# Later drains, squares and norms in the attention half of a two-layer encoder kernel

## The chip, the cores and the metric

One core of one Trainium2 chip runs the whole kernel in one launch. The metric is device time in microseconds (us). TensorE, VectorE, ScalarE, GpSimd and SyncE are called PE, DVE, ACT, POOL and SP, as in the profile; each runs its own instructions strictly in the order of its program, and waits on semaphores for the others. Line numbers are those of the kernel before, unless a line of after is named.

## The reference

Input x is 2048 rows of 1024 channels in float32. Layer A is a gated MLP that ends in x + mixer(x). Layer B, in which the change lies, is chunked attention, 16 heads of 64 channels:

```python
q, z = jnp.split(h @ w_qz, 2, axis=-1)        # h = rms_norm(x, b_norm_g)
sc = einsum('bqhd,bkhd->bhqk', q*scale, k) + rel_bias     # own chunk and the 8 before
o  = einsum('bhqk,bkhd->bqhd', softmax(sc), v)
x  = x + (o * silu(z)) @ w_out
return rms_norm(x, final_norm_g)
```

## The kernel before

The rows are worked on as four tiles t = 0..3 of 512 rows. The last 1100 us are layer B, tile by tile. A tile has eight head pairs p (names such as `pt3_14` are tile 3, head 14); a pair is walked in eight **score steps** u, four query blocks of each of its two heads. One pass of the loop over u (from L1883) does this:

- `score` (L1377), run two steps ahead: PE makes scores `s`, DVE adds the bias and takes the row maximum (L1400), ACT takes the exponential (L1407), DVE the reciprocal (L1410), POOL normalises into `pr` (L1411).
- `flip` (L1416): PE transposes `pr` in five 128x128 matmuls into the PSUM tile `tp` (L1427); ACT copies it to the high part of `pt` (L1431), DVE subtracts for the low part (L1432). There is one `tp` buffer, so the next transposition on PE waits for that DVE instruction.
- `value` (L1437), at u = 4 for the first head and at u = 0 of the next pair for the second: PE forms PV in tile `pv` (L1452). Then comes its **drain**: ACT copies half of it to `ot` (L1461), DVE adds it into `og32` (L1462), and after a pair's second head DVE gates with `Z` (L1469) and SP stores `og` (L1474). For the last two pairs `last_og` gates into `A_hh` instead (L1568).

Between these, PE is filled with slices of a generator: the projections `pj` of the next pair, whose weights are split into a high half on ACT (L229) and a low half on DVE (L230), and the **output products** `bo` of the tile before. These are a Strassen scheme in phases 1, 7, 2, 6, 5, 4, 3, each for two row pairs jp: three matmuls for each product (L112 to L114, high x high, low x high, high x low), right operands `wh_bo` and `wl_bo` (`whbo` and `wlbo` in the last tile), left operands split into `Sho`/`Slo` or `Qho`/`Qlo` (L338, L343).

`o_evict` (L1666) turns the phase products into output blocks (r, c) of 128x512: phases 2 and 5 give blocks (0,0) and (1,1): DVE adds the product to the residual rows `oc` loaded from `x1d` (L1760), POOL adds `ou` (L1762). Phases 4 and 3 give (1,0) and (0,1): DVE adds the product (L1780), then POOL adds the residual rows `or` that `fetch` loaded (L1782). `done` then appends the block's sum of squares on ACT (`jk`, L1694) to a list, `squares`, that the next score step empties, and its store to `x2d`. Once both blocks of a row group b exist, `finish` goes on the list `finals`: sum (`rr_f`, L1714), root (L126 on DVE, L127 on POOL) and reload `y` from `x2d`; the scaling by `r` and `gf` (L1732) and the store follow later. One entry of `finals` is taken in each score step.

The last tile has no tile behind it to hide its products: 13 slices of them lie in its last pair, the rest follow the last `value`. Its left operands come from `last_open` and `last_sums` (POOL, L1546 and L1557, tiles `A_hl`); `finish` runs at once and the rows `row0` to `row3` go straight to the output.

A list scheduler turns the order in which this code issues into one fixed order for each engine, by its own costs and by the ties of `on_beat` (after the last transposition). SP issues all DMAs of this part, in order, on eight lanes: a DMA waits for the one eight before it, and what stands behind it waits too. The 512-column buffers with tag C (`c_tile`, four of them) hold `oc`, `or` and the squares' output `jk`.

Of the kernel before, what the change touches and what calls it, by code (L numbers as in the profile page):

```python
# [22 lines left out]
NT = S // T  # L23
# [10 lines left out]
def trunk_kernel(  # L34
# [87 lines left out]
    sub, add = ALU.subtract, ALU.add  # L122
# [1150 lines left out]
    with ExitStack() as bctx:  # L1273
# [163 lines left out]
        def value(t, p, hd):  # L1437
# [6 lines left out]
            for i in blocks:  # L1444
                q0, q1 = max(0, i - 4), min(4, i + 1)
                for j in range(2):
                    o = j * 2560 + q0 * 512 + i * P
                    rhs = pt[:, o : o + P]
                    if q1 - q0 > 1:
# [4 lines left out]
                        start=(i == blocks[0] and j == 0), stop=(i == 7 and j == 1),  # L1454
                    )
            if hd == 0:
                og32s[t, p] = sb.tile([P, T], F32, tag="og32", name=f"og32_{t}_{p}", bufs=2)
# [20 lines left out]

        def square_all():
            while squares:  # L1480
                on_beat(squares.pop(0)())

        owed_out = []
# [49 lines left out]
        def last_open():  # L1533
# [17 lines left out]

            return [third] + last_sums(slice(0, 512)) + [lambda: all_of(slice(512, 768))]

# [112 lines left out]
        def o_evict(t):  # L1666
            xa, ya = {}, {}
            last = t + 1 == NT

            def resid(r, c, jp, x_):  # L1670
# [15 lines left out]
            def done(r, c, jp, y):  # L1686
# [11 lines left out]
                if last:  # L1698
                    square()
                else:  # L1700
                    squares.append(square)
                    send(x2d[t][b][:, c * 512 : c * 512 + 512], y)
                if (r, c) in ((1, 0), (0, 1)):
                    if last:
                        finish(b)
                    else:
                        finals.append(lambda: finish(b))

            def finish(b):
                send_all()  # L1710
                square_all()
                r = sm.tile([P, 1], F32, tag="rr", name=f"rr_f{t}_{b}", bufs=4)
# [35 lines left out]
            def evict(ph, jp, ps):  # L1748
# [6 lines left out]
                if ph in (2, 5):  # L1755
# [8 lines left out]
                    if ph == 5:  # L1764
                        tv(x_, ps, x_, op=add)
                        if last:
                            for r, c, y in ((1, 0, y_), (0, 1, x_)):
                                tg(y, y, place(r, c, jp), op=add)
                        elif jp:
                            fetch(1, 0, 0)  # L1770
# [6 lines left out]
                else:  # L1777
                    r, c, y = (1, 0, y_) if ph == 4 else (0, 1, x_)
                    o = place(r, c, jp) if last else y
                    tv(o, ps, y, op=add)  # L1780
                    if not last:
                        tg(y, y, rows.pop(0), op=add)  # L1782
# [84 lines left out]
        for t in range(NT):  # L1867
            for p in range(NPAIR):
# [14 lines left out]
                for u in range(8):  # L1883
# [9 lines left out]
                    elif u == 0 and before:  # L1893
                        value(*before, 1)
                    flip(t, p, u)
                    send_all()
                    square_all()
# [9 lines left out]
                before = t, p  # L1907
        value(*before, 1)
        run(gen)
        run(outs[NT - 1])  # L1910
# [57 lines left out]
```

## Time and profile before

| | |
|---|---|
| median of 3 runs | 2662.0 us (2661.07 to 2662.5) |
| the profiled execution | 2662.61 us, its span 2660.7 us, so 1.9 us lie around the span |
| mean granted PE clock | 0.997 |
| busy PE / DVE / ACT / POOL | 2606.8 / 1888.9 / 1302.4 / 897.6 us (98, 71, 49, 34% of the span) |
| recorded PE waits from 1557 us (the first `pv`) on | 19.8 us |
| matmuls, DVE, ACT, POOL instructions | 12960, 2944, 2303, 874 |

A row of the timeline gives start, duration, engine, line, operation, tiles written and read (buffer numbers left out), and in brackets the idle time before it with what ended that. A row of the waits gives engine, tile and line, what it waited for, then us in total, times, longest. DMA rows on SP are issues; the transfer itself follows.

### The profile page before, as it was taken

The page shows a single profiled execution, that of the slowest core. Times are in us where ns is not written, and L with a number is a line of the kernel's source. Part 1 is how long each engine was busy: PE and PEld are TensorE (multiplying, and loading weights), DVE is VectorE, ACT ScalarE, POOL GpSimd, SP SyncE. Part 2 cuts the span into 40 slices and gives each one's busy share as a digit, 9 for nine tenths or more (in the row PEclk, how much of TensorE's full clock was granted, in tenths as well). Part 3 has the DMA queues.
Part 4 walks back from the last instruction along what each step waited for, and adds up shares of the span by engine and source line. Part 5 has one row for each costly group of instructions (what it writes and reads, how often), then busy time and mean ns, then how long its engine had stood idle before and what let it go on. Part 6 is the DMA issues. An engine that isn't in the chain of part 4 may idle for free. (4 is left out here: it accounts for less than half of the span.)

```text
span 2660.7 us, 37988 instructions
## 1 busy us (share of the span) xinstructions
PE 2606.8 (98%) x12960; PEld 2182.1 (82%) x12960; DVE 1888.9 (71%) x2944; ACT 1302.4 (49%) x2303; POOL 897.6 (34%) x874
## 2 busy tenths in 40 slices
PE   9999999999999999999989999999999999999997
PEld 7788888888888888888878878888888888888886
DVE  5655667766677677757767767778778776877677
ACT  5422243443433434333356456666656655666564
POOL 3511335153252422203234434344333322332235
PEclk9999999999999999999999999999999999999999
DMA  8899999989888878968776587778788667765567
GB/s 299 307 333 332 348 363 325 326 306 358 314 312 296 316 241 323 327 205 270 276 251 218 183 277 237 232 241 269 236 280 276 206 199 225 248 221 159 190 221 260
DMA packets 273856, 718.72 MB, mean 270 GB/s; under 512 B 28800, under 2 KB 68736, under 8 KB 273664
## 3 DMA queue, kind: packets, MB, share of 16 engines
q1 hardware_dynamic: 273664, 716.31, 78.2%
q8 instruction: 103, 1.69, 0.3%
q14 instruction: 89, 0.73, 0.1%
HBM read 531.12 MB, written 174.59 MB: 265 GB/s over the span
## 5 line engine op out<-in xcount | busy, mean ns | idle before, releaser
L112 PE MATMUL P<-T,S 128*128 128x512 f32 x1248 | 495.1, 397 | 1.4 <-ACT S L435 1.4
L114 PE MATMUL P<-T,S 128*128 128x512 f32 x1248 | 489.4, 392 | 0.0
L113 PE MATMUL P<-T,S 128*128 128x512 f32 x1248 | 488.1, 391 | 0.6 <-DVE T L438 0.6
L1411 POOL TENSOR_SCALAR pr<-pr,sl 128x640 f32<-128x640 f32 (+4 forms) x256 | 209.4, 818 | 543.2 <-DVE sl L1410 474.6
L112 PE MATMUL pj<-hh_b,wh_b 128*128 128x512 f32 x768 | 319.2, 416 | 0.0
L114 PE MATMUL pj<-hh_b,wl_b 128*128 128x512 f32 x768 | 304.7, 397 | 0.6 <-DVE wl_b L230 0.5
L113 PE MATMUL pj<-hl_b,wh_b 128*128 128x512 f32 x768 | 302.6, 394 | 0.0
L1407 ACT ACTIVATE pr<-pr,nm 128x640 f32<-128x640 f32 (+4 forms) x256 | 195.4, 763 | 177.9 <-DVE nm L1400 176.0
L114 PEld LDWEIGHTS P<-T,S 128*128 128x128 f32 x1248 | 234.8, 188 | 50.3
L113 PEld LDWEIGHTS P<-T,S 128*128 128x128 f32 x1248 | 235.2, 188 | 46.2 <-DVE T L438 1.0
L112 PEld LDWEIGHTS P<-T,S 128*128 128x128 f32 x1248 | 235.2, 189 | 46.0 <-ACT S L435 1.7
L1432 DVE TENSOR_TENSOR pt<-tp,pt 128x640 fp32r<-128x640 f32 (+4 forms) x256 | 188.4, 736 | 43.0 <-ACT pt L1431 40.2
L1400 DVE CUSTOM_DVE_ANT_0 pr<-s,bias 128x640 f32<-128x640 f32 (+4 forms) x256 | 187.9, 734 | 38.7 <-PE s L1392 34.6
L1431 ACT CAST pt<-tp 128x640 fp32r<-128x640 f32 (+4 forms) x256 | 158.7, 620 | 52.5 <-PE tp L1427 49.5
L1427 PE MATMUL tp<-ident,pr 128*128 128x128 f32 x1120 | 167.1, 275 | 13.0 <-DVE pt L1432 10.0
L114 PEld LDWEIGHTS pj<-hh_b,wl_b 128*128 128x128 f32 x768 | 144.7, 188 | 34.5 <-DVE wl_b L230 2.2
L1427 PEld LDWEIGHTS tp<-ident,pr 128*128 128x128 f32 x1120 | 131.1, 141 | 47.8 <-issue 15.5
L1452 PEld LDWEIGHTS pv<-pt,V 128*128 128x128 f32 x896 | 143.6, 190 | 21.3 <-DVE pt L1432 6.0
L112 PEld LDWEIGHTS pj<-hh_b,wh_b 128*128 128x128 f32 x768 | 145.2, 189 | 17.6 <-ACT wh_b L229 1.2
L113 PEld LDWEIGHTS pj<-hl_b,wh_b 128*128 128x128 f32 x768 | 145.4, 189 | 16.9 <-DVE hl_b L187 0.4
L1452 PE MATMUL pv<-pt,V 128*128 128x256 f32 (+3 forms) x896 | 154.8, 320 | 3.2 <-DVE pt L1432 3.2
L230 DVE TENSOR_TENSOR wl_b<-raw_b,wh_b 128x1024 fp32r<-128x1024 f32 x96 | 120.0, 1251 | 24.3 <-ACT wh_b L229 23.5
(293 smaller groups left out, 5727.7 us busy)
## 6 DMA issues: line engine op xcount, KB each, us to landing
S<-hsd SPq DMA_DIRECT2D x288, 512.0 KB, 5.5
rw<-in_w_a SPq DMA_DIRECT2D x108, 512.0 KB, 6.3
A<-ytd SPq DMA_DIRECT2D x72, 512.0 KB, 5.8
raw_b<-wk SPq DMA_DIRECT2D x72, 512.0 KB, 4.1
hsd<-S SPq DMA_DIRECT2D x56, 512.0 KB, 4.4
V<-vhd SPq DMA_DIRECT2D x56, 512.0 KB, 5.0
bias<-reld SPq DMA_DIRECT2D x64, 320.0 KB, 3.9
va<-vd SPq DMA_DIRECT2D x32, 512.0 KB, 5.6
```

The costliest lines, as they stand in the source:

```text
L112: first = mm(ps, lh, rh, start=first, stop=False)
L113: mm(ps, lh, rl, start=False, stop=False)
L114: mm(ps, ll, rh, start=False, stop=last)
L230: tv(wl[:], raw[:], wh[:].bitcast(F32), op=sub)
L1400: nc.vector.tensor_tensor_reduce(out=pr[:, c0:].rearrange("p (a b) -> p a b", a=nseg), in0=ps[:, :nseg, :w], in1=bias[:, c0:].rearrange("p ...
L1407: nc.scalar.activation(pr[:, c0:], pr[:, c0:], AF.Exp, scale=-1.0, bias=nm[:], accum_out=sl[:])
L1411: nc.gpsimd.tensor_scalar(pr[:, c0:], pr[:, c0:], sl[:], 1.0, op0=ALU.mult, op1=ALU.mult)
L1427: ins = tpose(tp[:, b, :], pr[:, b * P : (b + 1) * P], ident[:])
L1431: nc.scalar.copy(oh, tp[:, b0:5, :].rearrange("p a b -> p (a b)"))
L1432: nc.vector.tensor_tensor(pt[:, 2560 + o + b0 * P : 2560 + o + 640], tp[:, b0:5, :].rearrange("p a b -> p (a b)"), oh.bitcast(F32), op=ALU ...
L1452: mm(po[:, q0 * P : q1 * P], vtl[t, p][:, i, hs], rhs, start=(i == blocks[0] and j == 0), stop=(i == 7 and j == 1),)
```

## The change

It does five things, all in layer B; no instruction is added or taken away (each engine issues as many as before), only their order differs.

1. The drain is cut out of `value` into its own function and put on a list; `drain_all` runs it behind `flip` of the same score step. Behind the last `value` it runs at once.
2. The squares of tiles 0 to 2 go through a second list, `young`, so they are issued two score steps after their sums, not one; `finish` empties both.
3. For tiles 0 and 1 an empty entry stands before `finish` in `finals`: the norm comes one step later.
4. In tile 2 (`at_once`) the residual rows of (1,0) and (0,1) are fetched in phase 5, and POOL adds them there (L1788 of after). Phases 4 and 3 then have only the DVE add.
5. In `last_open` an empty entry stands before `third` (L1546): its two POOL sums come one step later.

```diff
@@ value
+            drains.append(lambda: drain(t, p, hd, po))
+
+        drains = []
+
+        def drain_all():
+            while drains:
+                drains.pop(0)()
+
+        def drain(t, p, hd, po):
+            h = 2 * p + hd
             if hd == 0:
                 og32s[t, p] = sb.tile([P, T], F32, tag="og32", name=f"og32_{t}_{p}", bufs=2)
@@ squares
+        young = []
+
-        def square_all():
+        def square_all(every=False):
+            if every:
+                squares.extend(young)
+                young.clear()
             while squares:
                 on_beat(squares.pop(0)())
+            squares.extend(young)
+            young.clear()
@@ last_open
-            return [third] + last_sums(slice(0, 512)) + [lambda: all_of(slice(512, 768))]
+            return [lambda: None, third] + last_sums(slice(0, 512)) + [lambda: all_of(slice(512, 768))]
@@ o_evict
+            at_once = t + 2 >= NT
@@ done
-                    squares.append(square)
+                    young.append(square)
                     send(x2d[t][b][:, c * 512 : c * 512 + 512], y)
                 if (r, c) in ((1, 0), (0, 1)):
                     if last:
                         finish(b)
                     else:
-                        finals.append(lambda: finish(b))
+                        finals.extend([lambda: None, lambda: finish(b)][at_once:])
@@ finish
-                square_all()
+                square_all(True)
@@ evict, phase 5
                         tv(x_, ps, x_, op=add)
-                        if last:
+                        if at_once:
                             for r, c, y in ((1, 0, y_), (0, 1, x_)):
-                                tg(y, y, place(r, c, jp), op=add)
+                                if not last:
+                                    fetch(r, c, jp)
+                                tg(y, y, place(r, c, jp) if last else rows.pop(0), op=add)
                         elif jp:
                             fetch(1, 0, 0)
@@ evict, phases 4 and 3
                     tv(o, ps, y, op=add)
-                    if not last:
+                    if not at_once:
                         tg(y, y, rows.pop(0), op=add)
@@ the loop over u
                     flip(t, p, u)
+                    drain_all()
                     send_all()
@@ the end
         value(*before, 1)
+        drain_all()
         run(gen)
```

What it does to the engines' orders is seen at three places. The first is DVE in tile 0, where head 5's first transposition follows PV of head 4. Before:

```order
L230 TENSOR_TENSOR wl_b0_4_1_14506<-raw_b0_4_1_14504,wh_b0_4_1_14505 128x1024
L1462 TENSOR_TENSOR og32_0_2_14377<-pv0_4_14368,ot0_4_14378 64x512
L1432 TENSOR_TENSOR pt0_5_14381<-tp0_5_0_14382,pt0_5_14381 128x128
L1400 ISA pr0_5_3_14395,nm0_5_3_14396<-s0_5_3_14392,bias0_5_14173 128x512
L1400 ISA nm0_5_3_14396 128x1
```

With the change:

```order
L230 TENSOR_TENSOR wl_b0_4_1_14506<-raw_b0_4_1_14504,wh_b0_4_1_14505 128x1024
L1432 TENSOR_TENSOR pt0_5_14377<-tp0_5_0_14378,pt0_5_14377 128x128
L1472 TENSOR_TENSOR og32_0_2_14382<-pv0_4_14368,ot0_4_14383 64x512
L1400 ISA pr0_5_3_14395,nm0_5_3_14396<-s0_5_3_14392,bias0_5_14173 128x512
L1400 ISA nm0_5_3_14396 128x1
```

The low part of `pt` has changed places with the add of the drain. The same swap stands at the heads 3, 7, 9, 11 and 13 of this tile; the ACT order there (`ot`, then `pt`) is as it was.

The second is SP in tile 2, where the residual rows of tile 1's blocks are loaded: `oc1_111` for phase 5, `or1_...` for phases 4 and 3. Before, ahead of the store of `oc1_110`'s block:

```order
L276 DMA wh_bo1_4_1_21521<-ows4_1_103 128x1024
L276 DMA wl_bo1_4_1_21522<-ows4_1_103 128x1024
L1489 DMA x2d1_1_151<-oc1_110_21493 128x512
L1672 DMA oc1_111_21551<-x1d1_61 128x512
L1672 DMA or1_100_21558<-x1d1_61 128x512
L270 DMA raw_bo1_3_0_21851<-in_wb_out 128x1024
L177 DMA xr_b3_2_22008<-xtd3_141 128x4x256
L1489 DMA x2d1_3_153<-oc1_111_21551 128x512
L1672 DMA or1_101_21827<-x1d1_61 128x512
```

With the change the loads stand some forty DMAs further ahead, behind the bias load of head 10:

```order
L1484 DMA ogd2_144<-og2_3_20856 128x2x128 x2
L1369 DMA bias2_10_20951<-reld10_168 128x640
L1690 DMA oc1_110_21493<-x1d1_61 128x512
L1690 DMA oc1_111_21549<-x1d1_61 128x512
L1690 DMA or1_100_21556<-x1d1_61 128x512
L245 DMA raw_b2_6_0_21306<-wk6_0_82 128x1024
L1322 DMA Qh2_5_0_20915<-Qh2_5_0_20915 64x512
L1322 DMA Ql2_5_0_20916<-Ql2_5_0_20916 64x512
```

The load of `oc1_111` no longer stands behind the store `x2d1_1<-oc1_110`, which waits for POOL.

The third is the end, in the last tile. PE, around the first matmul of phase 6 (`bo_6_0`), before:

```order
L114 MATMUL bo_2_0_25531<-whbo_2_1_25313,Qlo_2_0_25451 128x512
L112 MATMUL bo_2_1_25561<-whbo_2_0_25307,Qho_2_1_25519 128x512
L113 MATMUL bo_2_1_25561<-wlbo_2_0_25308,Qho_2_1_25519 128x512
L112 MATMUL bo_6_0_25594<-whbo_6_0_25438,Qho_6_0_25546 128x512
L114 MATMUL bo_2_1_25561<-whbo_2_0_25307,Qlo_2_1_25520 128x512
L112 MATMUL bo_2_1_25561<-whbo_2_0_25307,Qho_2_1_25519 128x512
```

With the change:

```order
L114 MATMUL bo_2_1_25561<-whbo_2_1_25312,Qlo_2_1_25520 128x512
L112 MATMUL bo_2_1_25561<-whbo_2_1_25312,Qho_2_1_25519 128x512
L113 MATMUL bo_2_1_25561<-wlbo_2_1_25313,Qho_2_1_25519 128x512
L114 MATMUL bo_2_1_25561<-whbo_2_1_25312,Qlo_2_1_25520 128x512
L112 MATMUL bo_6_0_25594<-whbo_6_0_25438,Qho_6_0_25546 128x512
L113 MATMUL bo_6_0_25594<-wlbo_6_0_25439,Qho_6_0_25546 128x512
```

All twelve matmuls of `bo_2_1` now stand before the first of `bo_6_0`, where there were two. In the same way all twelve of `bo_3_0` now come before `bo_3_1`, where before five of `bo_3_1` stood ahead of the last five of `bo_3_0`. DVE's last rows before (`row2` and `row0` are the last two row groups):

```order
L1714 TENSOR_TENSOR rr_f3_3_25732<-ssq3_3_25678 128x1
L1780 TENSOR_TENSOR row0_25446<-bo_3_0_25740,ou3_1_0_25379 128x512
L126 TENSOR_SCALAR rr_f3_3_25732<-rr_f3_3_25732 128x1
L1732 SCALAR_TENSOR_TENSOR row3_25517<-row3_25517,rr_f3_3_25732,gf_13531 128x512 x2
L1714 TENSOR_TENSOR rr_f3_0_25756<-ssq3_0_25558 128x1
L1780 TENSOR_TENSOR row2_25448<-bo_3_1_25764,ou3_1_1_25419 128x512
L126 TENSOR_SCALAR rr_f3_0_25756<-rr_f3_0_25756 128x1
L1732 SCALAR_TENSOR_TENSOR row0_25446<-row0_25446,rr_f3_0_25756,gf_13531 128x512 x2
```

With the change:

```order
L1732 TENSOR_TENSOR rr_f3_3_25732<-ssq3_3_25678 128x1
L1800 TENSOR_TENSOR row0_25446<-bo_3_0_25740,ou3_1_0_25374 128x512
L126 TENSOR_SCALAR rr_f3_3_25732<-rr_f3_3_25732 128x1
L1750 SCALAR_TENSOR_TENSOR row3_25517<-row3_25517,rr_f3_3_25732,gf_13531 128x512 x2
L1732 TENSOR_TENSOR rr_f3_0_25756<-ssq3_0_25558 128x1
L126 TENSOR_SCALAR rr_f3_0_25756<-rr_f3_0_25756 128x1
L1800 TENSOR_TENSOR row2_25448<-bo_3_1_25764,ou3_1_1_25419 128x512
L1750 SCALAR_TENSOR_TENSOR row0_25446<-row0_25446,rr_f3_0_25756,gf_13531 128x512 x2
L1732 TENSOR_TENSOR rr_f3_2_25780<-ssq3_2_25591 128x1
```

The two small rows of `rr_f3_0` (L1714, L126; L1732 in after is the same code as L1714 before) have moved ahead of the last product's add into `row2`.

## The prediction

> **What bounds the kernel now.** First I read the busy times and the granted clock, then where PE waits from the first PV (1557 us) on, since the whole change lies behind it.
>
> ```profile
> PE 2606.8 (98%) x12960; PEld 2182.1 (82%) x12960; DVE 1888.9 (71%) x2944; ACT 1302.4 (49%) x2303; POOL 897.6 (34%) x874
> ```
>
> The waits of PE from 1557 us on, in total, times, longest:
>
> ```profile
> PE tp L1427 <- DVE pt L1432: 10.0, 17, 2.8
> PE pv L1452 <- DVE pt L1432: 3.2, 5, 1.8
> PE bo L112 <- ACT Qho L338: 1.6, 2, 1.3
> PE tp L1427 <- POOL A_hl L1557: 1.5, 1, 1.5
> PE s L1392 <- DVE nm L1400: 1.1, 2, 0.8
> PE bo L114 <- DVE rr_f L126: 1.0, 1, 1.0
> ```
>
> PE is busy 98% of the span, and the clock is full, so no instruction can be taken from DVE, ACT or POOL with profit except where PE waits for it. The change removes no PE instruction. All it can gain in front of PE's end is in this list, 18.4 us with four smaller rows 19.8; to that comes the chain behind PE's last matmul. Nearly all of it is PE held by a DVE instruction that is itself simply behind another in DVE's order. That is what a new order can mend, and also what it can make.
>
> A second view gives PE's busy time by stretch, to see where the list's waits lie:
>
> ```profile
> 2200.00:2300.00 100.00, 97.11 (x528) 83.30 (x527) 73.63 (x131) 58.27 (x107) 29.14 (x39) 0.98 0.73 232
> 2400.00:2500.00 100.00, 100.00 (x559) 86.92 (x558) 71.62 (x131) 60.07 (x110) 26.43 (x39) 1.00 0.58 186
> 2500.00:2600.00 100.00, 95.20 (x517) 80.56 (x516) 75.62 (x131) 58.27 (x105) 35.20 (x41) 1.00 0.64 210
> ```
>
> The first columns are the stretch, its length and PE's busy us. A stretch that runs undisturbed has nothing to give (100.0 from 2400 to 2500); the two dips, 2.9 and 4.8 us, are in the second half of tile 2 and in the last two pairs. So the sum goes place by place.
>
> **Term A: the drain behind the flip, tile 0.** Head 5's first transposition, in the timeline:
>
> ```profile
> 1607.34 0.58 ACT L1461 COPY ot<-pv 64x512 f32<-64x512 f32 x1
> 1607.35 1.22 DVE L230 TENSOR_TENSOR wl_b<-raw_b,wh_b 128x1024 fp32r<-128x1024 f32 x1 [1.17 <-ACT wh_b L229]
> 1607.94 0.27 ACT L1431 CAST pt<-tp 128x128 fp32r<-128x128 f32 x1
> 1608.49 0.68 DVE L1462 TENSOR_TENSOR og<-pv,ot 64x512 f32<-64x512 f32 x1
> 1609.09 0.27 DVE L1432 TENSOR_TENSOR pt<-tp,pt 128x128 fp32r<-128x128 f32 x1
> 1609.51 0.41 PE L1427 MATMUL tp<-ident,pr 128*128 128x128 f32 x2 [0.77 <-DVE pt L1432]
> ```
>
> ACT's part of `pt` is done at 1608.21, so with the swap DVE can start its part at 1608.49, 0.60 sooner. PE's 0.77 shrinks to 0.17. The same pattern gives these waits between 1600 and 1720:
>
> ```profile
> PE tp L1427 <- DVE pt L1432: 2.1, 5, 0.8
> ```
>
> Five waits, the other four below 0.6, which vanish: 2.1 - 0.17, so **1.9 us**. In the other tiles most drains keep their places in the orders of ACT and DVE, so I count nothing there; the PE waits of tiles 1 and 3 at these points are mostly nil, which hides a loss as well as a gain of 0.7.
>
> **Term B: the norm a step later, tile 1.**
>
> ```profile
> 1991.36 0.16 DVE L1714 TENSOR_TENSOR rr_f<-ssq 128x1 f32<-128x1 f32 x1 [1.15 <-ACT jk L1694]
> 1992.18 0.50 PE L114 MATMUL bo<-wh_bo,Slo 128*128 128x512 f32 x1 [1.00 <-DVE rr_f L126]
> ```
>
> DVE idles 1.15 us for a square, with `Slo` behind it, and PE waits 1.00 for that. In the new order `rr_f0_1` stands two steps later: **1.0 us**. The scalings move with it, and their reloads and stores pass other DMAs on SP. I cost that at nothing, since those are for the next pair and used a step or more later; without that cover it would be a wait like PV's 1.8 below.
>
> **Term C: squares and residual loads, tile 2.** SP, DVE, and PE's waits from 2245 to 2335:
>
> ```profile
> 2248.01 0.32 SPq L1489 DMA_DIRECT2D x2d<-oc  x1
> 2248.38 0.42 SPq L1672 DMA_DIRECT2D oc<-x1d  x1
> 2253.48 0.69 DVE L1760 TENSOR_TENSOR oc<-bo,oc 128x512 f32<-128x512 f32 x1 [2.26 <-DMA oc<-x1d]
> PE pv L1452 <- DVE pt L1432: 2.4, 3, 1.8
> PE tp L1427 <- DVE pt L1432: 1.5, 3, 0.6
> ```
>
> The load of `oc1_111` is issued at 2248.38, right behind a store that waits for POOL, and lands five us later. DVE stands 2.26 us, `pt` is behind it, and PV waits 1.8. With the load some forty DMAs ahead this goes: **1.8 us**. Of the other 2.1 us in the stretch (2.4 - 1.8 + 1.5) I see two waits whose DVE neighbours change and take **0.4**, between 0 and 2.1.
>
> The price of those earlier loads is on SP. In tile 2 they now stand here:
>
> ```profile
> 2187.49 0.51 SPq L1369 DMA_DIRECT2D bias<-reld  x1
> 2192.92 0.33 SPq L245 DMA_DIRECT2D raw_b<-wk  x1
> ```
>
> SP has 5.4 us of room there, three issues of 0.4 fit, and their C buffers are due back from a square two steps behind. I cost it at nothing; the room's far end is a rival below.
>
> **Term D: the last pair.**
>
> ```profile
> 2585.07 2.76 DVE L1568 SCALAR_TENSOR_TENSOR A_hh<-og,Z 128x256 f32<-128x256 f32 x2
> 2584.84 2.71 POOL L1546 TENSOR_TENSOR A_hl<-A_hh 128x512 f32<-128x512 f32 x2
> 2588.83 0.63 PE L1427 MATMUL tp<-ident,pr 128*128 128x128 f32 x4 [2.76 <-DVE pt L1432]
> 2622.92 0.76 DVE L1568 SCALAR_TENSOR_TENSOR A_hh<-og,Z 128x256 f32<-128x256 f32 x2
> 2587.07 1.04 ACT L1609 CAST whbo<-raw_bo 128x1024 fp32r<-128x1024 f32 x1 [1.43 <-DMA raw_bo<-in_wb_out]
> 2590.28 0.67 ACT L1431 CAST pt<-tp 128x640 fp32r<-128x640 f32 x1
> 2626.44 0.50 PE L112 MATMUL bo<-whbo,Qho 128*128 128x512 f32 x1 [1.28 <-ACT Qho L338]
> ```
>
> The gating pair takes 2.76 us beside POOL's two `third` sums and 0.76 without them. In the new order `pt3_14_0` stands ahead of the pair and `third` a step later, so the wait of 2.76 at 2588.83 goes. But ACT is in order: the cast of `whbo_1_0` still cannot start before its load lands at 2587.07, and behind it stand a split, a square, an exponential and the cast of `pt3_14_1`, at 2590.3 as before. That transposition's DVE part then ends near 2591.8, when PE, ahead by 2.76, has waited since about 2590.2. So of 2.76 us only **2.0** are kept; DVE's wait of 0.82 for the same tile is in that. The later waits of this pair I leave as they are.
>
> At 2626.44 `bo_6_0` waits 1.28 for the chain drain, POOL sums, `Qho_6_0`. In the new order ten more matmuls of `bo_2_1` stand ahead, 2.3 us of work at 0.23 us apart (the first two rows of term E): **1.3 us** saved.
>
> The Trainium skill, page "SBUF — State Buffer", section "Who interferes with whom", has a rule for this pair: a DVE instruction with two SBUF inputs and a GpSimd instruction that reads SBUF share a port under an exclusive lock, and the one that comes second stands still until the other is through. The trace agrees in direction (2.76 beside 2.71 of POOL, 0.76 alone). By that rule the pair costs 2.76 wherever POOL reads beside it and term D stays as it is, since `pt3_14_0` has gone ahead of the pair; but it speaks against part 4 of the change, which is the rival on POOL's adds.
>
> **Term E: behind the last matmul.**
>
> ```profile
> 2650.78 0.39 PE L113 MATMUL bo<-wbo,Qho 128*128 128x512 f32 x1
> 2651.01 0.39 PE L114 MATMUL bo<-wbo,Qlo 128*128 128x512 f32 x1
> 2651.26 1.41 DVE L1732 SCALAR_TENSOR_TENSOR row<-row,rr_f,gf 128x512 f32<-128x512 f32 x2 [0.66 <-POOL rr_f L127]
> 2652.66 0.68 DVE L1780 TENSOR_TENSOR row<-bo,ou 128x512 f32<-128x512 f32 x1
> 2656.40 1.42 DVE L1732 SCALAR_TENSOR_TENSOR row<-row,rr_f,gf 128x512 f32<-128x512 f32 x2 [0.66 <-POOL rr_f L127]
> ```
>
> PE ends at E = 2651.4; the last scaling starts 5.0 us later, since the add of `row2` stands behind the scaling of `row3` (1.41) and row 0's norm and scaling come behind that. In the new order `bo_3_0` ends twelve matmuls (2.8 us) ahead of E, so row 3 is scaled by about E + 0.1, `row2` added by E + 0.9, row 0 (its root done meanwhile) scaled by E + 2.4, and row 2's root of 0.9 us follows: the last scaling at E + 3.3. **1.7 us**. If row 3 comes a step later, 0; at best 2.1.
>
> **The sum.** 1.9 + 1.0 + 1.8 + 0.4 + 2.0 + 1.3 + 1.7 = 10.1 us. Against it stands what I cannot see: the schedule has changed around some dozen other places, in which an in-order engine may now wait in front of a transposition. The nearest row is PV's 1.8; I take one such wait, and bounds of none and of three with POOL's and SP's prices below. 10.1 - 1.8 = 8.3 us. The profiled execution took 2662.6 (span 2660.7 and 1.9 around it); the median of runs is 0.6 below that. 2662.6 - 8.3 gives 2654.3, on the median's scale 2653.7: I say **2654**.
>
> **The rivals.**
>
> *The next wait takes it back.* PE is at 98%, DVE's order stays as dense, and term D showed how a gain of 2.76 loses 0.76 to the next cast. If A and D lose all but a fifth in this way (5.2 to 1.0) and two waits of 1.8 are added, 10.1 - 4.2 - 3.6 = 2.3 remains: 2660. For it: seventeen waits of one kind, each behind the one before. Against: the stretches between have nothing due for 10 us and more, so a gain is not caught up with. Chance 0.18.
>
> *POOL's adds beside DVE's splits.* Part 4 puts four POOL adds of tile 2 into phase 5, beside DVE's weight splits, and a POOL add is a 1.3 us instruction (2.71 for two). If each holds up a split with PE behind it, 4 x 1.3 = 5.2 us: 8.3 - 5.2 = 3.1, so 2659. Against it: the adds also leave phases 4 and 3, where they stood beside splits too. By the Trainium skill's rule (page "SBUF — State Buffer", the section named above) each of them would hold a split for the add's whole length. Chance 0.08.
>
> *SP stands still, and the kernel is slower.* The loads of `oc` and `or` now wait for C buffers which the squares release, up to two score steps later. A step lasts 6.7 us in this row pair:
>
> ```profile
> 2581.93 0.81 DVE L1400 CUSTOM_DVE_ANT_0 pr<-s,bias 128x640 f32<-128x640 f32 x1
> 2588.60 0.81 DVE L1400 CUSTOM_DVE_ANT_0 pr<-s,bias 128x640 f32<-128x640 f32 x1
> ```
>
> If a buffer comes back two steps late (13.3 us) where SP has 5.4 us of room, the K, Q and weight transfers behind are 7.9 us late, and PE stands for them. One such place gives 10.1 - 7.9 = 2.2, so about 2660; at two of the three tiles 2668. It decides from two places on. For it: a queue in order of eight lanes, and the loads moved far ahead of their use. Against: the squares of phases 2 and 5 are over a step before the new place of the loads. Chance 0.12 for slower.
>
> *The order does not change what is waited for.* ACT's order of `ot` and `pt` is the same nearly everywhere, so the drain's move may do only term A. With A alone and a wait added, 2662. Chance 0.06.
>
> **How the numbers follow.** My forecast has 0.56: it holds between 10.1 + 2.1 + 1.8 + 1 (all uncertain parts good, no new wait), near 2647, and 2657. Rivals: 0.18 at 2660, 0.08 at 2659, 0.12 at 2668 (most of it from 2663 up), 0.06 at 2662. The range of 2647 to 2666 leaves out some 0.06 below and 0.1 above. Within 0.2%, which is 5.3 us and about what a measurement of this kernel tells from no change, lie the first two rivals, the last one, and a part of SP's first place. Faster by more: the forecast and a little of the rivals, 0.6. Slower by more: 0.13. The same: 0.27.
>
> **What would show it.** A: in tile 0 the waits of `tp` between 1600 and 1720 fall from 2.1 to about 0.2. B: no row `bo <- rr_f`. C: no DVE idle of over 1 us for `oc`, PV's wait of 1.8 gone, and no stretch of SP with late K or weights. D: the DVE pair of L1568 at 1.7 us or less, or with no transposition behind it; the third transposition of head 14 about 2.0 us earlier; no wait of `bo_6_0`. E: the last scaling 3.3 us after PE's end, not 5.0. The prediction is wrong if the sum of PE's waits from the first PV on falls by less than 4 us or if a new group of waits over 2 us stands in it.

## The result, and the profile after

The changed kernel takes **2656.4 us** (median of 22 runs, 2653.0 to 2663.2), the kernel before, run beside it on the same chips, 2661.1 (22 runs, 2656.8 to 2666.8). The ratio is 0.9983, with a 95% interval from 0.9977 to 0.9988: some 4.5 us, a sixth of one per cent. The prediction said 2654 on a scale where before was at 2662.0, a gain of 8.3 by its sum. The direction and the range hold; of the size about half came. Measured by the 0.2% (5.3 us) within which the prediction calls a time the same, the gain lies there, and to that outcome it had given 0.27.

Busy times of the kernel after:

```profile
PE 2607.8 (98%) x12960; PEld 2180.7 (82%) x12960; DVE 1889.9 (71%) x2944; ACT 1303.1 (49%) x2303; POOL 897.0 (34%) x874
```

The busy times of PE, DVE, ACT and POOL move by 1.0 us or less, that of the weight loads (PEld) by 1.4. So the difference is looked for in waits. Those of PE from 1557 us on, after (in total, times, longest):

```profile
PE tp L1427 <- DVE pt L1432: 8.6, 16, 1.1
PE bo L113 <- DVE wbo L1627: 1.3, 2, 0.7
PE s L1392 <- DVE nm L1400: 1.2, 2, 0.7
PE bo L113 <- DMA wl_bo<-ows: 0.9, 1, 0.9
PE pv L1452 <- DVE pt L1432: 0.9, 2, 0.5
PE pj L114 <- DVE wl_b L230: 0.9, 2, 0.6
PE tp L1427 <- DVE rr_f L1732: 0.8, 1, 0.8
PE tp L1427 <- POOL pr L1411: 0.7, 1, 0.7
PE pv L1452 <- ACT pt L1431: 0.5, 1, 0.5
```

Beside before's list: the rows of `Qho` (1.6), of POOL's `A_hl` (1.5) and of `rr_f` ahead of a product (1.0) are gone, PV's wait went from 3.2 to 0.9, the longest from 2.8 to 1.1. But the waits for `wbo` (0.2 in before) and `wl_bo` (0.4) have grown, and four rows are new. One of these, POOL's `pr`, stands at 1561.80, ahead of the first PV, which is at 1563.32 here; before has the same wait at 1555.93. In sum 19.8 us have become 15.8, and 15.1 from the first PV on. The kernel did lose its long waits; a good part of them came back as short ones elsewhere.

One row must be known before the profiles are compared. The profiled execution of after took 2663.2 us (span 2661.4), more than that of before (2662.6, span 2660.7), though the median is lower. In it stands this, in layer A, far ahead of everything that the change touches:

```profile
785.35 0.58 PE L113 MATMUL mx<-vl,ws 128*128 128x256 f32 x1 [3.95 <-DVE vl L438]
```

Another execution of the same kernel (the last experiment below) does not have it and spans 2654.7. So I compare by **lead**: the start of the same matmul in both kernels, with the first PV of layer B (1557.44 us in before) as the common zero. Below, minus is ahead of before. The columns are after, after in that second execution, the parts of the change alone (numbered as in the section on the change), and before in a second execution:

```
us in before, matmul           after  again |  1     2     3     4   | before again
1591.97 PV of head 3, tile 0   +0.3   -0.3  | +0.3   0.0   0.0  +0.5 |   0.0
1745.83 PV of head 15, tile 0  -0.9   -1.1  |  0.0  -0.4  +0.2  +0.5 |  -0.2
1997.65 bo0_3_1, tile 1        -3.0   -2.2  | +0.9  -2.3  -1.3  +2.1 |  +0.6
2087.49 tp2_2_3                -1.0   -1.3  | +1.1  -3.1  +0.7  +3.0 |  +0.3
2219.11 tp2_10_0               -0.5   -1.0  | +0.9  -2.7  +0.8  +3.3 |  +0.1
2344.84 tp3_0_3                -4.5   -5.0  | +0.5  -6.8  -2.8  +1.8 |  +0.2
2564.74 tp3_13_0               -4.2   -4.8  |  0.0  -6.6  -2.8  +1.4 |  -0.2
2634.32 bo_5_0                 -6.1   -7.4  | -0.1  -8.1  -2.9  +0.2 |  -0.2
2651.01 last matmul            -4.8   -6.2  | -0.1  -6.4  -2.9  -0.3 |  -0.2
last matmul to last scaling     5.02   5.08 |  5.38  4.50  5.38  6.13|   5.39
```

Before repeats itself within 0.6 us at every mark, after within 1.3, but chance is larger than these two pairs show. The kernel of part 4 has before's order on every engine up to 2480 us, and yet it is 3.3 behind at 2219. Two of the kernels below (all but part 4, and that one with the last adds shared) have one order up to 2632 us, and differ by up to 2.9 at the marks up to 2565. From one mark to the next, executions of one order differ by up to 1.6 us. So only a step of 2 us or more between neighbouring marks is taken for a fact of the kernel here, and a smaller one where it comes in every kernel that has the part.

One source of chance is PE's clock. Its granted share drops to a half for 3.4 us, once or twice between the first PV and the last matmul in twelve of the fourteen profiled executions, and in neither execution of after. The matmuls of 512 columns then start 0.43 us apart instead of 0.23; in one kernel (squares in a scratch of their own) a spell at 2621.6 cost 1.6 us of lead. Before has one at 2256.9, in tile 2, and part 4's kernel, with the same order, has none there. The columns are those of the view by stretch in the prediction, the granted clock is the third from the right; before, then part 4's kernel:

```profile
2240.00:2260.00 20.00, 18.23 (x93) 15.66 (x93) 12.91 (x25) 10.92 (x21) 6.78 (x8) 0.92 0.78 243
2260.00:2280.00 20.00, 18.59 (x106) 16.32 (x107) 15.23 (x29) 11.91 (x22) 4.76 (x7) 1.00 0.77 235
```

At the last matmul after is 4.8 us ahead, and the chain behind it is 0.4 shorter, which makes 5.2 (6.5 in the second execution); the medians say 4.5, between 3.2 and 6.1 by the interval.

The places, in the order of the terms. Tile 0, head 5's first transposition (5.6 us later on the clock than in before, whose first PV came 5.9 earlier), and PE's waits from 1600 to 1720:

```profile
1615.12 0.41 PE L1427 MATMUL tp<-ident,pr 128*128 128x128 f32 x2 [0.17 <-DVE pt L1432]
PE tp L1427 <- DVE pt L1432: 0.2, 1, 0.2
```

0.77 became 0.17 and 2.1 became 0.2, both as forecast, yet the lead over these heads moved by far less (below).

The border to tile 2, on POOL, ACT, DVE and PE:

```profile
2007.06 1.29 POOL L1802 TENSOR_TENSOR ou<-ou,or 128x512 f32<-128x512 f32 x1 [1.98 <-DMA or<-x1d]
2008.38 0.63 ACT L1712 ACTIVATE jk<-ou 128x512 f32<-128x512 f32 x1 [2.48 <-POOL ou L1802]
2009.02 1.03 ACT L186 CAST hh_b<-xr_b 128x1024 fp32r<-128x1024 f32 x1
2010.08 1.23 DVE L187 TENSOR_TENSOR hl_b<-xr_b,hh_b 128x1024 fp32r<-128x1024 f32 x1 [2.00 <-ACT hh_b L186]
2012.49 0.50 PE L114 MATMUL pj<-hh_b,wl_b 128*128 128x512 f32 x1 [0.64 <-DVE wl_b L230]
```

A square on ACT stands 2.48 us for POOL's residual add, which itself stands for a load; behind the square is the first cast of the next tile's input, behind that DVE's low half (idle 2.00), and then PE. The order is that of before, where ACT stood 1.42:

```profile
2003.85 0.63 ACT L1694 ACTIVATE jk<-ou 128x512 f32<-128x512 f32 x1 [1.42 <-POOL ou L1782]
2004.48 1.03 ACT L186 CAST hh_b<-xr_b 128x1024 fp32r<-128x1024 f32 x1
```

New is that PE waits at its end. Counted from the first PV, POOL's add comes 1.35 us sooner than in before, and PE had come 3.0 sooner. Here the lead of 3.0 falls to 1.0.

Tile 2, the block whose load was late before (DVE), and PE's waits from 2245 to 2335:

```profile
2254.64 0.69 DVE L1778 TENSOR_TENSOR oc<-bo,oc 128x512 f32<-128x512 f32 x1
PE tp L1427 <- DVE pt L1432: 1.7, 2, 0.9
```

No idle time ahead of it (2.26 before), and the row of PV's waits (2.4) is gone. In the view by stretch:

```profile
2200.00:2300.00 100.00, 99.19 (x548) 85.50 (x547) 74.58 (x136) 59.97 (x110) 30.88 (x40) 1.00 0.72 226
2500.00:2600.00 100.00, 96.47 (x522) 81.00 (x521) 75.70 (x133) 59.36 (x107) 38.20 (x43) 1.00 0.65 210
```

PE's 97.1 of before became 99.2, with the clock at 1.00 instead of 0.98; the stretch before the end, 95.2, only 96.5.

The last pair, on DVE and PE:

```profile
2587.45 0.82 DVE L1432 TENSOR_TENSOR pt<-tp,pt 128x640 fp32r<-128x640 f32 x1
2588.20 2.02 DVE L1585 SCALAR_TENSOR_TENSOR A_hh<-og,Z 128x256 f32<-128x256 f32 x2
2588.43 0.73 PE L1427 MATMUL tp<-ident,pr 128*128 128x128 f32 x5 [0.39 <-DVE pt L1432]
2594.37 0.41 PE L1427 MATMUL tp<-ident,pr 128*128 128x128 f32 x2 [0.89 <-DVE pt L1432]
```

`pt3_14_0` now stands ahead of the pair, and the 2.76 are 0.39; at the transposition after it PE waits 0.89. The waits of PE from 2580 on:

```profile
PE tp L1427 <- DVE pt L1432: 3.6, 5, 1.1
```

`bo_6_0` waits no more, but now the products of phase 3 wait 1.3 for the split of their weights, `wbo` (0.2 in before). The end on POOL, DVE and PE:

```profile
2641.89 5.24 POOL L1788 TENSOR_TENSOR ou<-ou,row 128x512 f32<-128x512 f32 x3
2644.27 3.94 DVE L1627 TENSOR_TENSOR wbo<-raw_bo,wbo 128x1024 fp32r<-128x1024 f32 x2
2646.05 0.50 PE L113 MATMUL bo<-wbo,Qho 128*128 128x512 f32 x1 [0.71 <-DVE wbo L1627]
2648.27 0.50 PE L113 MATMUL bo<-wbo,Qho 128*128 128x512 f32 x1 [0.56 <-DVE wbo L1627]
2649.62 1.41 DVE L1750 SCALAR_TENSOR_TENSOR row<-row,rr_f,gf 128x512 f32<-128x512 f32 x2
2652.07 0.39 PE L114 MATMUL bo<-wbo,Qlo 128*128 128x512 f32 x1
2652.42 1.41 DVE L1750 SCALAR_TENSOR_TENSOR row<-row,rr_f,gf 128x512 f32<-128x512 f32 x2 [0.66 <-POOL rr_f L127]
2657.09 1.41 DVE L1750 SCALAR_TENSOR_TENSOR row<-row,rr_f,gf 128x512 f32<-128x512 f32 x2 [0.66 <-POOL rr_f L127]
```

PE ends at 2652.5, and the last scaling starts 4.6 us later, not 3.3.

### The profile page after: what moved, and what is told of

It is laid out like the page before. It is cut to its first block, busy times and chain, and to the rows that moved or that the text cites. A ratio compares the mean times of both kernels' runs of the same rounds, so it can differ in the third digit from the quotient of the medians.

```text
span 2661.4 us, 37994 instructions
## 1 busy us (share of the span) xinstructions
PE 2607.8 (98%) x12960; PEld 2180.7 (82%) x12960; DVE 1889.9 (71%) x2944; ACT 1303.1 (49%) x2303; POOL 897.0 (34%) x874
```

## The experiments

The theory after the result: the squares (part 2), which take the C buffers, are the whole gain; the waits that the other parts mend are taken back at once. The rivals: every part pays its own term as the prediction had it; or the drain and the delayed `third` (parts 1 and 5) make the gain of the last pair. Parts 1 to 4 are each done alone, parts 3 and 4 are taken out of the change, and two suspected costs are taken away by themselves. Part 5 alone, and parts 1 and 5 without part 2, were not run.

**Part 1 alone, the drain behind the flip.**

```diff
+            drains.append(lambda: drain(t, p, hd, po))
...
                     flip(t, p, u)
+                    drain_all()
```

> Only part 1: the drain behind the flip. Theory (each part acts only at its own place, and what the trace of after shows at a place is that part's): tile 0's odd heads only, PE about 1.1 us ahead by the end of tile 0, nothing gained later, wait of 2.8 before head 14's second transposition of the last tile still there: 2660, ratio 0.9995. Rival (the drain is what frees the transpositions everywhere, the last pair too): that wait gone, 3 us or more, 2658 or less.

2661.6 us against 2662.0, ratio 1.0001 [0.9992, 1.0010]: nothing. PE's waits for `tp` from 1600 to 1720 are 0.2 here too, so the edit does what it says, and the lead does not follow: +0.3 at head 3, 0.0 at head 15. PE around the mended wait in this kernel shows why:

```profile
1608.53 0.41 PE L1427 MATMUL tp<-ident,pr 128*128 128x128 f32 x2 [0.19 <-DVE pt L1432]
1609.94 0.40 PE L114 MATMUL pj<-hh_b,wl_b 128*128 128x512 f32 x1
1610.35 0.33 PE L1392 MATMUL s<-K,Qh 128*128 128x128 f32 x1
```

and the same last two instructions in before:

```profile
1610.92 0.39 PE L114 MATMUL pj<-hh_b,wl_b 128*128 128x512 f32 x1
1611.15 0.22 PE L1392 MATMUL s<-K,Qh 128*128 128x128 f32 x1
```

The transposition starts 0.98 earlier than in before (1608.53 against 1609.51), the score behind it 0.80 earlier: it now starts 0.41 behind the product ahead of it, where 0.23 is the pace. The gap of 0.18 is not written as a wait, for the product ahead is recorded until 1610.34. The next transposition is 0.68 earlier (1611.39 against 1612.07), the next PV 0.57 (1617.02 against 1617.59), which is hardly more than the 0.43 that PV of head 4 had had (1604.28 against 1604.71). A wait of 0.58 was mended and 0.14 kept. In the last pair the wait of 2.8 is still there:

```profile
PE tp L1427 <- DVE pt L1432: 2.9, 2, 2.8
```

So term D isn't the drain's.

**Part 2 alone, the squares two steps behind.**

```diff
-                    squares.append(square)
+                    young.append(square)
...
+            squares.extend(young)
+            young.clear()
```

> Only part 2: squares two steps behind. Theory: this part moves the loads of the residual rows in tile 2 ahead (PV's wait of 1.8 gone, some 3 to 4 us at 2250 to 2310), puts the last pair's pt ahead of the gating pair and bo_2_1 ahead of bo_6_0 (2 us), and takes the wait for rr_f (1 us): 6 us, 2655, as much as the whole change. Rival (the parts are needed together, the squares alone only move an engine with room): within 2 us of before.

2656.7 us, ratio 0.9985 [0.9976, 0.9993]: as much as the whole change, within the intervals. Its lead is the larger one from 2087 us on (-8.1 at `bo_5_0`). PE's waits from 2245 to 2335 in this kernel:

```profile
PE tp L1427 <- DVE pt L1432: 1.4, 2, 0.8
PE pv L1452 <- DVE pt L1432: 0.5, 1, 0.5
```

and from 2580 on:

```profile
PE tp L1427 <- DVE pt L1432: 2.7, 2, 1.9
PE bo L113 <- DVE wbo L1617: 1.7, 2, 1.0
```

The wait of 2.8 behind the pair and that of `bo_6_0` are gone without parts 1 and 5: the second rival falls. Whether parts 1 and 5 would do it too without part 2 is not known; part 1 alone does not. The new wait for `wbo` is there as well, so it is not a cost of part 4. In the order of this kernel `pt3_14_0` stands ahead of the pair, though nothing in that place was edited; the list scheduler arrives at it from the moved squares. The chain behind the last matmul is shorter too, 4.50 instead of 5.39.

**Part 3 alone, the norm a step later.**

```diff
-                        finals.append(lambda: finish(b))
+                        finals.extend([lambda: None, lambda: finish(b)][at_once:])
```

> Only part 3: the norm of tiles 0 and 1 a step later. Theory: the wait of 1.0 for rr_f at 1992 goes, PE 1.3 to 1.9 us ahead at 1995, and this is given back at the border to tile 2, since the load of the last residual rows lands no sooner: total 0 to 1 us, 2660.5. Rival (the give-back belongs to the squares, not to the border's load): the 1.3 to 1.9 us stay, 2659.5.

2660.7 us, ratio 1.0001 [0.9992, 1.0010]: nothing. The column shows a gain of 1.5 up to 1998 us and 2.0 given back by 2087, at the same border as in after. The expectation had said so, and why: the last residual load lands no sooner (counted from the first PV, POOL's add behind it starts 0.6 later than in before). It had not foreseen that the lead of this one execution grows by 3.6 in tile 2, though `oc1_111` is loaded as late as in before (issued at 2250.02, right behind the store; DVE stands 1.62 for it). There is no spell at half clock in that place here, and PE's waits from 2245 to 2335 are 2.2 instead of 3.9. The time of the runs shows none of it.

**Part 4 alone, the residual sums of tile 2 in phase 5.**

```diff
-                        if last:
+                        if at_once:
                             for r, c, y in ((1, 0, y_), (0, 1, x_)):
-                                tg(y, y, place(r, c, jp), op=add)
+                                if not last:
+                                    fetch(r, c, jp)
+                                tg(y, y, place(r, c, jp) if last else rows.pop(0), op=add)
...
-                    if not last:
+                    if not at_once:
                         tg(y, y, rows.pop(0), op=add)
```

> Only part 4: tile 2's residual sums in phase 5. Theory: nothing in tile 3 before its last pair, and in the last 15 us the new order of the end (twelve matmuls of bo_3_0 first, the second split ahead of row 3's add) makes PE wait over 1 us for wbo_3 while the chain behind PE's end shortens by 0.4: about 1 us slower, 2662. Rival (my term E): the shorter chain wins, 1.7 us faster, 2659.5.

2662.0 us, ratio 1.0002 [0.9993, 1.0011]: nothing. Neither the wait for `wbo` that was expected is there, nor term E's gain: the chain behind the last matmul is longer, 6.13 instead of 5.39. Its order is neither before's nor after's: the last add stands behind the scaling of a third row (2657.16).

**All but part 4.**

> The change without part 4 (residual sums of tile 2 as before). Theory: part 4 does nothing for PE before the last pair, and the end's order as before costs about as much as the new one (PE waits 1.7 instead of 1.3 for wbo_3, the chain behind the last matmul 4.5 instead of 5.0 us): the same as the whole change within 1 us, 2656 to 2657. Rival (part 4 carries tile 2's gain): 2 to 4 us slower than the whole change.

2658.7 us against 2662.6, ratio 0.9985 [0.9976, 0.9994]. By the interval it is the same as the whole change (0.9983). The end is shorter without part 4 (4.48 from the last matmul to the last scaling instead of 5.02), but PE waits longer for `wbo`: 1.7 instead of 1.3. DVE's two splits of those weights show both:

```profile
2640.57 1.71 DVE L1627 TENSOR_TENSOR wbo<-raw_bo,wbo 128x1024 fp32r<-128x1024 f32 x1
2644.64 1.21 DVE L1627 TENSOR_TENSOR wbo<-raw_bo,wbo 128x1024 fp32r<-128x1024 f32 x1
```

They stand apart, with a row's sum and add between them; in after they are one block of 3.94, the second ahead of that sum and add. PE gets its second split sooner that way, and DVE's rows come later.

**POOL's last adds shared with DVE**, on top of that: of the four sums of phase 5 in the last tile, those of block (0,1) go to DVE.

```diff
-                                tg(y, y, place(r, c, jp), op=add)
+                                (tv if r == 0 else tg)(y, y, place(r, c, jp), op=add)
```

> As e5, and in the last tile's phase 5 the two adds into ou3_1_0 and ou3_1_1 on DVE instead of POOL. Theory (the end gives its gain back because DVE's splits of wbo_3 run beside POOL's adds): the splits back to 1.2 us each, PE's waits for wbo_3 fall from 1.7 to below 0.7, 1 to 1.5 us faster than e5. Rival (the splits are simply late, behind ACT's casts): they stay late, and DVE has two more adds of 0.7 in front of them: e5 or up to 1 us slower.

2658.7 us, ratio 0.9981 [0.9972, 0.9990]. DVE's splits of the last weights, in this kernel:

```profile
2638.40 1.21 DVE L1627 TENSOR_TENSOR wbo<-raw_bo,wbo 128x1024 fp32r<-128x1024 f32 x1
2641.04 1.21 DVE L1627 TENSOR_TENSOR wbo<-raw_bo,wbo 128x1024 fp32r<-128x1024 f32 x1
```

Beside POOL's sums two of them took 3.94 in after, and 1.71 and 1.21 without part 4; here, with POOL done, each takes 1.21. PE's wait for them falls from 1.7 to 1.1:

```profile
PE bo L113 <- DVE wbo L1627: 1.1, 1, 1.1
```

So POOL's adds are part of that wait, some 0.6 of 1.7. Below 0.7 and a gain of 1 to 1.5 us were expected; 1.1 is left, and the time is that of the kernel without these adds shared (2658.7 both). Why the rest stays was not tested.

**Before, with a scratch of its own for the squares.** Only the squares' output, which nothing reads, is taken out of the C buffers (it is BF16 in a buffer of its own):

```diff
-                    jk = c_tile(f"jk{t}_{r}{c}{jp}")
+                    jk = half_tile("J", f"jk{t}_{r}{c}{jp}", 1, BF16)
```

> Before, with the output of the squares (which nobody reads) in a buffer of its own, 512 columns of bfloat16, not in one of the four C buffers; the squares stay where they were. Theory (later squares help because the loads of the residual rows get their C buffers sooner): the loads stand far ahead, no wait of PV for them in tile 2, 2 to 4 us faster, 2658 to 2660. Rival (later squares help because ACT has no square ahead of a cast that PE waits for): no gain, 2662.

2658.3 us, ratio 0.9990 [0.9980, 1.0000]. The squares stay one step behind their sums; only the loads are free of them. PE's waits from 2245 to 2335, here:

```profile
PE tp L1427 <- DVE pt L1432: 0.9, 1, 0.9
PE pv L1452 <- DVE pt L1432: 0.5, 1, 0.5
```

The lead goes from -1.0 at 2219 to -5.5 at 2345, a step like after's, and like that of every kernel with the loads ahead (4.0 to 4.5 in nine executions). In the last pair both waits stay (2.6 behind the pair, `Qho` 1.3), and the lead falls by 2.2 from 2565 to 2634, 1.6 of it in the spell at half clock named above. So loads that stand further ahead mend tile 2, whichever way they get there, whatever the clock's share in the step is (below); the last pair isn't mended by them.

**Before, once more.**

> The kernel before, unchanged, profiled once more, to see how steady its waits are. Theory: the waits at 1992 (rr_f, 1.0), 2255 (PV, 1.8) and 2588 (2.8) come again within 0.5 us, so that they may be read from one profile. Rival: the first two, which end on DMA landings, move by 1 us or more from profile to profile.

A span of 2662.5. Its lead against the first execution stays within 0.6 us at all marks. The three waits come again with 1.0, 2.0 and 2.7, but the first is put down to `Slo`, which stands right behind `rr_f`.

**Parts 1, 2 and 5, without the norm and the residual.**

> The change without parts 3 and 4. Theory (what is gained at 1992 is lost again at the border to tile 2 because, with the norm a step later, the cast of hh_b stands on ACT behind a square that waits for the last residual load; without part 3 this square stands behind the cast): PE keeps its lead at the border (about 3 us at 2040, as the squares alone) and the whole is 1 to 2 us faster than with part 3, 2655. Rival (the lead at the border is lost to the load itself, whatever stands behind it): lead at 2040 about 1 us, 2657 as before.

2655.2 us against 2661.3, ratio 0.9981 [0.9972, 0.9990]. At the border to tile 2, on ACT:

```profile
2000.32 1.05 ACT L186 CAST hh_b<-xr_b 128x1024 fp32r<-128x1024 f32 x1
2005.87 0.64 ACT L1711 ACTIVATE jk<-ou 128x512 f32<-128x512 f32 x1
```

Here the cast of the next tile's input stands ahead of the square, no wait for `wl_b` appears, and the lead is kept: -1.7 at 1998, -2.5 from 2040 to 2087. With the whole change it fell from -3.0 to -1.0 there. So it is part 3 that gives its own gain back. The later squares put the cast ahead (part 2 alone has it so too); with the norm a step later the square stands ahead of that cast again, as in before. All five executions with part 3 lose 0.9 to 2.1 at this border; the four that have part 2 without it gain 0.8.

**The same with POOL's last adds shared.**

> As e9, and the two adds of the last tile's phase 5 on DVE (as in e6). Theory: e9 and 0.5 us more from the end, since the splits take 1.2 us each instead of 1.7 and 1.2: 2654.5, the fastest of the set. Rival: nothing more than e9.

**2653.5 us** against 2661.3, ratio 0.9973 [0.9964, 0.9982]: the fastest of all, 0.27% below before. Its interval overlaps that of the whole change (0.9977 to 0.9988) and that of the kernel before this one (0.9972 to 0.9990), so that it beats either is not shown. It leaves the norm and the residual sums as they were.

**Own scratch, squares, `third` and the shared adds (parts 2 and 5).**

> Parts 2 and 5, the squares' output in a buffer of its own, and the two adds on DVE. Theory (later squares and the own buffer help tile 2 by the same means, sooner C buffers): no more in tile 2 than either alone (lead at 2415 of 5.5 to 6.8 us), and with the last pair about 2654 to 2656. Rival (they are two separate gains that add): lead at 2415 of 9 us or more, 2652 or less.

2656.2 us, ratio 0.9976 [0.9964, 0.9988]. The lead grows by 4.1 in tile 2, to -6.0 at most, as with the squares or the scratch alone: the two are one gain, and don't add.

**After, once more.**

> The changed kernel once more, one look, to see how steady its profile is. Theory: the wait of 3.9 us at 785 us, in layer A, which the change does not touch, belongs to that one execution and is absent, and the leads in layer B come again within about 1 us. Rival: it is there again, so the new kernel has it for good.

A span of 2654.7, and no row of 3.95 in layer A. The leads agree with the first execution within 1.3 us, the chain at the end is 5.08.

## Why the prediction was half right

By its own terms, as lead gained over each term's stretch, in the two executions of after:

```
term                                   predicted   after   again
A  tile 0, head 3 on                        1.9     1.1     0.8   (0.9 and 1.1 from the first PV on)
B  norm, tile 1 and the border              1.0     0.1     0.2
C  loads of tile 2                          2.2     3.5     3.7
D  last pair                                3.3     1.7     2.4
E  behind the last matmul                   1.7     0.4     0.3
a new wait: bo_5_0 to the last matmul      -1.8    -1.3    -1.3   (others within the rows above)
sum                                         8.3     5.2     6.5   (A from the first PV on; rows are rounded)
```

**A: the wait was right, its worth was not.** The waits fell exactly as said, from 2.1 to 0.2. But the prediction took a wait that goes for time that is won. With the drain alone the lead between head 3 and head 15 moved by 0.3 us: at the place shown the rest went into gaps of 0.1 to 0.2 us that no list of waits names. That heads 1 to 3 moved by more than 1 us to and fro (-1.4 at PV of head 1, and back by 1.0 or more at head 3, in all six kernels with the drain) was not in the prediction at all.

**B: right at its place, and given back 20 us later.** Neither a row `bo <- rr_f` nor one for `Slo` is left, and the lead grows by 2.2 and 1.1 at 1998. The failing step is that the gain was taken as kept, with the norm's move "at nothing": the prediction looked at SP's queue for what the moved norm passes. The next thing that PE needs hangs on the last residual load, by way of POOL's sum, the square and the cast, and it does not come sooner by as much. Without part 3 the cast is ahead of the square and the lead stays.

**C: right mechanism and right waits, and more time than waits.** The buffers that the squares hold were what kept the loads back; the own scratch shows it without touching any square's order. Of 3.9 us of waits from 2245 to 2335, 1.7 remain, so 2.2 went, just what the prediction has (1.8 and 0.4). The lead grew by 4.0 between 2219 and 2345 in both executions. The surplus is of the size of before's spell at half clock at 2256.9, 3.4 us long: part 4's kernel, which has before's order here but no spell, gains 1.5 on before in this stretch. The prediction read the clock as full, though its own row for 2200 to 2300 has 0.98. The spell stands there in three of the five executions with the late load, those in which PV waited 1.8 to 2.0; it is missing in the two with 1.1 and 1.5, and in all nine with the early load. But the 2.76 at 2588 brought none in before. Whether the long wait brings the spell, so that its end belongs to the change, is not shown; as far as the prediction goes, the surplus is luck.

**D: right waits, half to three quarters of the size.** The prediction read the new place of `pt3_14_0` off the order and did not say which part of the change puts it there. The squares do: with part 1 alone the wait of 2.8 stays, with part 2 alone it is gone. And where the prediction let one transposition behind it wait again, for 0.8, there are five waits of that kind from 2580 on, 3.6 us in sum. The Trainium skill (page "SBUF — State Buffer", section "Who interferes with whom") says of a DVE instruction and a GpSimd one that share the port that the second stands still. The pair took 2.02 here beside POOL's sums of `third` (2.72), against 0.76 alone in before. That agrees with the rule's direction. No transposition stood behind the pair; the scores for which DVE works next waited 0.47 (at 2591.02). So the place of the pair counts for more than its length.

**E: the right way, a fifth of the size, and a new wait ahead of it.** The prediction read the tail from the order alone, with the last scaling at E + 3.3. It had row 3 scaled by E + 0.1, because `bo_3_0` ends 2.8 us ahead of E. PE did that; DVE was not there. The two splits of `wbo` stood from 2644.27 to 2648.2, beside POOL's adds, and the sums and adds of the rows came behind them: the scaling ahead of row 3's runs from 2649.62, row 3's starts at 2652.42, at E itself, so the last add and the last scaling come 1.3 us later than forecast. Part 2 alone shortens the tail to 4.50, and so does the change without part 4 (4.48); with part 4 it is 5.02 in after and, in another order, 6.13 alone. So part 4 lengthens the tail, by 0.5 to 0.7. On PE's side the splits made the wait of 1.3, which part 2 alone has as well (1.7): what PE won at `bo_6_0` was handed to the next thing that it needs. What the order of part 4 gives with POOL silent was not tried, so how the 1.3 us of the tail divide between the splits' place and their length stays open.

In the prediction's words, the rival "the next wait takes it back" came true at the border to tile 2 and at the end, and not in tile 2 or the last pair. "POOL's adds beside DVE's splits" was right about the engines and wrong about the place: not tile 2's sums in phase 5, but those of the last tile, which the change did not touch. In before, PE waited 0.2 for those splits, though one of them took 2.25 beside POOL's adds.

The rival in which SP stands still fell: with the whole change no K, Q or weight transfer shows up among PE's waits but one of 0.9 (`wl_bo`, 0.4 in before). The rule set beforehand, that the prediction is wrong if PE's waits fall by less than 4 or a new group of over 2 us stands among them, does not strike, the first half by little: 19.8 became 15.8 (15.1 from after's own first PV on), and the largest group that has come up is `wbo` with 1.3.

Why, with the later squares, a delayed norm makes the list scheduler put a square ahead of the cast is not settled; the orders show that it does. Nor is the difference of parts 3 and 4 to nothing: with and without them the intervals overlap. That part 2 alone is the whole gain holds within the intervals too (0.9976 to 0.9993 against 0.9977 to 0.9988): a microsecond or two from the other parts would not show.

## What to carry to other kernels

A wait in the list is not what mending it is worth: follow the lead, the start of the same instruction in both kernels, to the next two or three things that the bound engine needs, and look at the granted clock beside it. Before a step of the lead is explained, compare executions whose order is the same up to there; here they were up to 3 us apart. A buffer that an unneeded output shares with a load is worth looking for first: here one line that gave this output its own buffer brought a ratio of 0.9990 [0.9980, 1.0000], against 0.9983 for the whole change. At the end of a program work out the tail on every engine that has a queue there, for once the first wait goes, PE can wait for a split that POOL's adds slow, as it did for 1.3 us here and 0.2 before.

## What the runs showed of the hardware

A DVE subtraction of 128x1024 takes 1.21 us with POOL idle. Beside POOL's f32 sums two took 3.94, and single ones 1.22 (part 4's kernel), 1.71 (all but part 4) and 2.25 (before). POOL's sum of 128x512 lasts 1.3 us alone, and 5.24 for three beside DVE's two splits, so both sides stretch.

PE's granted clock can drop to a half for 3.4 us in the midst of a kernel that keeps PE busy for 98% of its span. It comes and goes between executions of one order, and cost some 1.5 us in the two places where it was followed (2256.9 in before, beside part 4's kernel, and 2621.6 with the scratch).

Single executions of one kernel differ by up to 10 us (2653.0 to 2663.2 for after), and one part of that is a wait of 3.95 us in code that both kernels share, present in one profile and absent in the next. A change of 4 us can't be judged by one profile's span. The lead counted from a mark right ahead of the change is better, but executions of one order were still up to 1.6 us apart from one mark to the next, and 3.3 in sum.
